# First stage of a one-core diffusion layer: order of the first loads, the split of the modulation product, and the first rows' high parts

## The chip, the cores and the metric

The kernel runs on one core of one Trainium2 chip. The metric is the device time of one execution in microseconds. The kernel before takes 2886.26 us in the median of three runs (2884.76 to 2886.59).

Names of the engines: PE is TensorE (matrix products and transposes through PSUM), DVE is VectorE, ACT is ScalarE, POOL is GpSimd, SP is the engine that only issues transfers (most loads here; ACT and POOL issue some as well). SBUF is the on-chip memory with 128 partitions, PSUM the accumulators that PE writes.

## What is computed

One layer of a diffusion backbone for 256 context tokens and 2048 latent tokens of width 1024, all in float32. Cut to what the first stage needs:

```python
def adaln(cvec, w_mod, b_mod):
    m = jax.nn.silu(cvec) @ w_mod + b_mod
    return jnp.split(m[:, None, :], 6, axis=-1)      # sh1, sc1, g1, sh2, sc2, g2

sh1, sc1, g1, sh2, sc2, g2 = adaln(c_ctx[None, :], w_mod[l], b_mod[l])
h = rms_norm(xp, norm1_g[l]) * (1 + sc1) + sh1
q, k, v, f = project(h, w_in[l], q_norm_g[l], k_norm_g[l])
...
sh1, sc1, g1, sh2, sc2, g2 = adaln(c, w_mod[l], b_mod[l])
h = rms_norm(xs, norm1_g[l]) * (1 + sc1) + sh1
```

`w_mod` is 1024 x 6144; the first 2048 of its columns give the shift and scale that stand ahead of the first projection. `w_in` is 1024 x 2048. After it come differential attention over 2560 keys, a Fourier mixing, an output projection and a squared-ReLU MLP; the change doesn't touch them.

## The kernel before

The tokens are 18 row blocks of 128; blocks 0 and 1 are the context. A float32 product is made from three faster ones: both operands are split into a high part (a cast to the type fp32r) and a low part (what the cast left), and high x high, high x low and low x high are accumulated (`mm3`, L88 to L90). The high part of W is cast by ACT, the low part subtracted by DVE.

The part that matters here is written by hand, in an order that the scheduler doesn't change (`tc.manual_schedule`, L437 to L547). Each engine and each issuing queue works through its own instructions in that order and stops at one whose inputs aren't there yet.

- `setup_small` (L92 to L110) loads the conditioning vectors c and c_ctx and the bias b_mod on SP's queue and the gains norm1_g, norm2_g and subln_g on ACT's, as rows of one tile; makes silu of the first 16 rows; transposes the tile on PE (L107) and copies it to `cols` (L108). `cols` then holds a column for each group of 128 values.
- `load(0)` brings row block 0 (X[0], 512 KB). Then come the eight pieces wm0 to wm7 of W_mod (L444), each 128 x 2048, 1 MB; X[1] is loaded between wm2 and wm3. ACT's queue also carries two pieces `rp` of the rotary table (L283), 64 KB each, which later stages use.
- `norm` (L204 to L212): square and row sum on ACT, the mean on DVE (nss, L209), the power -1/2 on POOL (nrs, L85), the scaling on DVE. Here of block 0; of block 1 at step 4 of the next loop.
- The transposes of block 0 on PE (L451), into two PSUM tiles of four.
- The modulation product, eight steps of k. PE multiplies the two columns of c and c_ctx with 1536 columns of wm_k (three products of 512, L455), and DVE sums the other 512 columns for each of the two vectors (L459 and L461), partition by partition.
- Six pieces of W, halves of 512 KB (L474), go where wm0 to wm2 were. There are 16 halves and six buffers, so the others are issued as the splitting frees buffers.
- The product's rows are copied from PSUM (L482) and transposed to columns (L484); sixteen products with a vector of ones (L489) sum DVE's part over the partitions. Bias (L492) and `mk_scale` (L201, L202) give `modc` and `scale1`. POOL loads the gains of q and k and the lambda vectors (L113, L116).
- Block 0 is modulated straight from its transposes in PSUM, the first tile by ACT (L502) and the second by DVE (L500), into SBUF; DVE then makes its high parts (L510) and low parts (L511). The transposes of block 1 follow on PE (L515).
- Projection of block 0: for each of eight k, ACT casts the four column groups of W (L523), DVE subtracts (L524), PE makes 12 products. On the side ACT modulates block 1 (L502, at k = 1 to 4), its high and low parts are made at k = 5 (L531, L532), and block 2 is normalised at k = 6; its transposes stand on PE within the last step (L221).
- Afterwards the four groups of block 0 are used (f: L402, v: L377, squares of q and k: L271) while PE projects block 1.

The pools of PSUM: `pj` has four tiles of 128 x 512 (the projection's groups, and the modulation product before them), `pt` two tiles for transposes, `pg` and `pm` one each.

## Time and profile before

| what | before |
|---|---|
| median of three runs | 2886.26 us (2884.76 to 2886.59) |
| the profiled execution's own time | 2886.51 us |
| its span in the trace | 2884.7 us |
| PE busy | 2847.6 us, 99% |
| DVE busy | 2011.5 us, 70% |
| ACT busy | 1547.0 us, 54% |
| POOL busy | 1061.7 us, 37% |
| moved by DMA | 492.93 MB, 171 GB/s over the span |

Times in the trace count from the start of the span. A row of the timeline gives start, duration (both us), engine, line, operation, output and inputs with their shapes, how many instructions were joined (x), and in brackets how long the engine had been idle before and what released it. A row of the groups gives line, engine and operation, then count, busy time in all (us), mean of one (ns), and idle time ahead of them with what ended most of it. A row of waits names the engine and line that waited, what for, us in total, times, and the longest.

### The profile page before, as it was taken

The page shows a single profiled execution, that of the slowest core. Times are in us where ns is not written, and L with a number is a line of the kernel's source. Part 1 is how long each engine was busy: PE and PEld are TensorE (multiplying, and loading weights), DVE is VectorE, ACT ScalarE, POOL GpSimd, SP SyncE. Part 2 cuts the span into 40 slices and gives each one's busy share as a digit, 9 for nine tenths or more (in the row PEclk, how much of TensorE's full clock was granted, in tenths as well). Part 3 has the DMA queues.
Part 4 walks back from the last instruction along what each step waited for, and adds up shares of the span by engine and source line. Part 5 has one row for each costly group of instructions (what it writes and reads, how often), then busy time and mean ns, then how long its engine had stood idle before and what let it go on. Part 6 is the DMA issues. An engine that isn't in the chain of part 4 may idle for free.

```text
span 2884.7 us, 43207 instructions
## 1 busy us (share of the span) xinstructions
PE 2847.6 (99%) x15119; PEld 2468.6 (86%) x15119; DVE 2011.5 (70%) x3375; ACT 1547.0 (54%) x3503; POOL 1061.7 (37%) x869
## 2 busy tenths in 40 slices
PE   8999999999999999999999999999999999999999
PEld 4888787688888888888889999999998888888887
DVE  6676776898988989865477777778775353345554
ACT  4333322798998989853356565556554332232221
POOL 1112112699999999942223333333332000000000
PEclk9999999999999999999999999999999999999999
DMA  7777888521211312037777677667747464345663
GB/s 283 202 201 190 227 210 231 195 106 43 73 69 45 114 38 98 21 112 208 236 219 233 219 247 229 220 218 238 232 166 254 146 201 137 133 143 185 200 206 110
DMA packets 392779, 492.93 MB, mean 171 GB/s; under 512 B 26467, under 2 KB 306384, under 8 KB 389490
## 3 DMA queue, kind: packets, MB, share of 16 engines
q1 hardware_dynamic: 387136, 479.73, 52.7%
q0 software_dynamic: 1872, 7.28, 0.7%
q10 hardware_dynamic: 3554, 3.17, 0.4%
q8 instruction: 119, 1.95, 0.3%
q14 instruction: 98, 0.80, 0.1%
HBM read 312.58 MB, written 179.59 MB: 171 GB/s over the span
## 4 chain that ended last, share of the span: by engine, by line
PE 91%; DVE 3%; ACT 3%; DMA 2%; issue 1%; POOL 0%; SPq 0%; ACTq 0%; DVEq 0%; POOLq 0%
PE Ss L1022 10%; PE ps L88 8%; PE ps L89 8%; PE ps L90 8%; PE pts L1077 5%; PE po L90 4%; PE po L88 4%; PE po L89 4%; PE pj L88 4%; PE pj L89 4%; PE pj L90 4%; PE pA L1685 2%; PE pA L1686 2%; PE pB L1685 2%; PE pB L1686 2%; PE pB L1687 2%
## 5 line engine op out<-in xcount | busy, mean ns | idle before, releaser
L1027 DVE TENSOR_REDUCE mxs<-Ss 128x1 f32<-128x512 f32 x636 | 413.3, 685 | 63.1 <-PE Ss L1022 52.0
L1362 DVE TENSOR_TENSOR sl<-sr,sh 128x768 fp32r<-128x768 f32 x168 | 161.7, 964 | 337.8 <-ACT sh L1361 337.3
L1062 POOL TENSOR_TENSOR P0s<-P0s,P1s 128x1024 f32<-128x1024 f32 (+2 forms) x128 | 378.7, 2958 | 10.7
L1361 ACT CAST sh<-sr 128x768 fp32r<-128x768 f32 x168 | 140.2, 836 | 424.8 <-PE ps L89 424.8
L1727 POOL TENSOR_TENSOR gs<-g,g 128x384 f32<-128x384 f32 x48 | 69.6, 1451 | 469.8 <-ACT g L1697 410.8
L1046 ACT ACTIVATE P1s<-Ss,mxs 128x512 f32<-128x512 f32 x318 | 215.2, 694 | 36.1 <-DVE mxs L1030 36.1
L88 PE MATMUL pj<-wh,hh 128*128 128x512 f32 x576 | 229.4, 398 | 3.9 <-DVE qn L289 3.2
L89 PE MATMUL ps<-tlT,sh 128*128 128x512 f32 x585 | 229.3, 392 | 0.0
L88 PE MATMUL ps<-thT,sh 128*128 128x512 f32 x585 | 229.0, 391 | 0.0
L89 PE MATMUL pj<-wl,hh 128*128 128x512 f32 x576 | 228.5, 397 | 0.5 <-DVE wl L524 0.5
L90 PE MATMUL ps<-thT,sl 128*128 128x512 f32 x585 | 227.7, 389 | 0.0
L90 PE MATMUL pj<-wh,hl 128*128 128x512 f32 x576 | 227.3, 395 | 0.0
L1046 ACT ACTIVATE P0s<-Ss,mxs 128x512 f32<-128x512 f32 x318 | 214.1, 691 | 5.5 <-DVE mxs L1030 4.9
L1022 PE MATMUL Ss<-KS1s,Qs 128*128 128x512 f32 x636 | 196.2, 420 | 6.2 <-ACT P0s L1046 3.5
L1022 PE MATMUL Ss<-KS0s,Qs 128*128 128x512 f32 x636 | 195.5, 420 | 2.4 <-ACT P1s L1046 2.4
L1077 PEld LDWEIGHTS pts<-ident,P0s 128*128 128x128 f32 x1280 | 157.7, 140 | 42.8 <-issue 2.1
L1077 PE MATMUL pts<-ident,P0s 128*128 128x128 f32 x1280 | 190.5, 272 | 0.7 <-ACT P1s L1046 0.7
L1696 ACT ACTIVATE g<-uz 128x384 f32<-128x384 f32 x144 | 75.8, 527 | 201.0 <-DVE uz L1719 171.3
L1061 POOL TENSOR_SCALAR P1s<-P1s,tots 128x1024 f32<-128x1024 f32 (+2 forms) x128 | 171.7, 1342 | 5.8
L1089 DVE TENSOR_TENSOR als<-pts,ahs 128x512 fp32r<-128x512 f32 x256 | 165.9, 681 | 6.8 <-ACT ahs L1084 6.6
L88 PE MATMUL ps<-ophT,sh 128*128 128x512 f32 x423 | 165.7, 392 | 1.1 <-DVE uz L1719 1.1
L90 PE MATMUL ps<-ophT,sl 128*128 128x512 f32 x423 | 165.7, 392 | 0.0
(531 smaller groups left out, 8056.3 us busy)
## 6 DMA issues: line engine op xcount, KB each, us to landing
sr<-sd SPq DMA_DIRECT2D x84, 768.0 KB
a<-in_w SPq DMA_DIRECT2D x184, 256.0 KB
sd<-gs SPq DMA_DIRECT2D x192, 192.0 KB
sd<-g SPq DMA_DIRECT2D x144, 192.0 KB
wm<-in_w_mod SPq DMA_DIRECT2D x32, 512.0 KB
Qs<-qd SPq DMA_DIRECT2D x32, 512.0 KB
b<-in_w SPq DMA_DIRECT2D x64, 256.0 KB
b<-tsum SPq DMA_DIRECT2D x64, 256.0 KB
```

The source lines that it names most:

```text
L88: nc.tensor.matmul(ps, lh, rh, start=first, stop=False)
L89: nc.tensor.matmul(ps, lh, rl, start=False, stop=False)
L90: nc.tensor.matmul(ps, ll, rh, start=False, stop=last)
L1022: nc.tensor.matmul(S[:, :w], self.Q[:, x, m, j * P:j * P + P], self.hd.KS[m][:, b * 512:b * 512 + w], start=(x == 0), stop=(x == 1))
L1027: nc.vector.tensor_reduce(self.mx[j][:, m, b:b + 1], self.S[j, m, b], axis=AX.X, op=ALU.max)
L1046: nc.scalar.activation(dst, S, AF.Exp, bias=self.mx[j][:, m, 6:7], accum_out=self.sm[j][:, m, b:b + 1])
L1061: nc.gpsimd.tensor_scalar(p, p, tot[:, 3:4], 0.0, op0=ALU.mult, op1=ALU.add)
L1062: nc.gpsimd.tensor_add(d, d, p)
L1077: nc.tensor.transpose(pt[:, c:c + P], self.p0[j][:, (kb + t) * P:(kb + t + 1) * P], ident)
L1089: nc.vector.tensor_sub(t, self.pt[kb], f32(self.A[kb][0]))
L1361: nc.scalar.copy(hi, src)
L1362: nc.vector.tensor_sub(lo, src, f32(hi))
```

## The change

W_mod's first two pieces lead SP's queue, x0 comes behind them, and x1 behind the second half of W. c and c_ctx are loaded on ACT's queue and are transposed by themselves (16 rows, `setup_cond`); the bias and the gains are loaded afterwards, on ACT's queue too (`load_rows`), and transposed after step 1 of the modulation product (`setup_rows`). Block 0 is normalised at step 2 and transposed at steps 3 to 6, block 1 normalised in the second stage, at step 1.

In the modulation product PE takes 1280 columns of each piece (512, 512, 256) and DVE 768. DVE's sums are reduced by two transposing reduces, and four products with shifted identity blocks (`quads`, which a later stage used already) finish the sum over the partitions, where sixteen products with ones stood.

ACT casts the four groups of W's first piece, and DVE subtracts the first, ahead of the scale. For block 0, `h_first` lets ACT write the high part straight from PSUM and DVE write the whole value to SBUF from the same PSUM tile, then subtract; the first tile ahead of the projection's loop, the second at its step 1. Block 1's transposes are made in two fours after steps 1 and 3, its modulation is at steps 2 to 5, its split at step 6. Block 2 is loaded at step 4 and normalised at step 7. In the last step the groups go 3, 2, 0, 1.

```diff
@@ -89,23 +89,33 @@
-        def setup_small(pool, pps):
+        def load_cond(pool):
             rows = pool.tile([P, P], F32, tag="t2", name="rows", bufs=6)
             nc.vector.memset(rows, 0.0)
-            nc.sync.dma_start(rows[0:8, :], a["c"].rearrange("o (r p) -> (o r) p", p=P))
-            nc.sync.dma_start(rows[8:16, :], a["c_ctx"].rearrange("(r p) -> r p", p=P))
-            nc.sync.dma_start(rows[32:80, :], a["b_mod"].rearrange("o (r p) -> (o r) p", p=P))
-            nc.scalar.dma_start(rows[80:88, :], a["norm1_g"].rearrange("o (r p) -> (o r) p", p=P))
-            nc.scalar.dma_start(rows[88:96, :], a["norm2_g"].rearrange("o (r p) -> (o r) p", p=P))
-            nc.scalar.dma_start(rows[96:97, :], a["subln_g"])
+            nc.scalar.dma_start(rows[0:8, :], a["c"].rearrange("o (r p) -> (o r) p", p=P))
+            nc.scalar.dma_start(rows[8:16, :], a["c_ctx"].rearrange("(r p) -> r p", p=P))
+            return rows
+        def setup_cond(pool, pps, rows):
             e = pool.tile([16, P], F32, tag="t2", name="e", bufs=6)
             nc.scalar.activation(e, rows[0:16, :], AF.Exp, scale=-1.0)
             nc.vector.tensor_scalar_add(e, e, 1.0)
             nc.vector.reciprocal(e, e)
             nc.vector.tensor_mul(rows[0:16, :], rows[0:16, :], e)
+            pr = pps.tile([P, 16], F32, tag="pg", name="prc")
+            nc.tensor.transpose(pr, rows[0:16, :], ident[0:16, 0:16])
+            nc.vector.tensor_copy(cols[:, 0:16], pr)
+        def load_rows(rows):
+            nc.scalar.dma_start(rows[32:80, :], a["b_mod"].rearrange("o (r p) -> (o r) p", p=P))
+            nc.scalar.dma_start(rows[80:88, :], a["norm1_g"].rearrange("o (r p) -> (o r) p", p=P))
+            nc.scalar.dma_start(rows[88:96, :], a["norm2_g"].rearrange("o (r p) -> (o r) p", p=P))
+            nc.scalar.dma_start(rows[96:97, :], a["subln_g"])
+        def setup_rows(pps, rows):
             pr = pps.tile([P, P], F32, tag="pg", name="pr")
             nc.tensor.transpose(pr, rows, ident)
-            nc.vector.tensor_copy(cols, pr)
+            nc.vector.tensor_copy(cols[:, 32:97], pr[:, 32:97])
             nc.vector.tensor_scalar_mul(cols[:, 96:97], cols[:, 96:97], 1.0 - LAM_INIT)
...
@@ -169,13 +179,17 @@
-        def mod_sums(t2, pps, sums, gi):
-            z = t2(f"quad{gi}")[:, 0:224]
+        def quads(t2, nm):
+            z = t2(nm)[:, 0:224]
             nc.gpsimd.memset(z, 0.0)
             nc.gpsimd.tensor_add(z[:, 96:128], ident[:, 0:32], ident[:, 32:64])
             for q in (2, 3):
                 nc.gpsimd.tensor_add(z[:, 96:128], z[:, 96:128], ident[:, 32 * q:32 * q + 32])
+            return z
+        def mod_sums(t2, pps, sums, gi):
+            z = quads(t2, f"quad{gi}")
             FIN[gi] = pm = pps.tile([P, 4, 2, 4], F32, tag="pm", name=f"pm{gi}")
             for q in range(4):
                 nc.tensor.matmul(pm, z[:, 96 - 32 * q:224 - 32 * q], sums[:, :, :, q::4], start=(q == 0), stop=(q == 3))
@@ -436,31 +450,36 @@
             with tc.manual_schedule():
                 with tc.tile_pool(name="p0r", bufs=3) as rows, tc.tile_pool(name="p0m", bufs=KD - 3, side="right") as more:
-                    setup_small(p1, pps)
-                    load(0)
+                    rw = load_cond(p1)
                     wm = []
                     for k in range(KD):
                         wm.append((rows if k < 3 else more).tile([P, 2048], F32, tag="row", name=f"wm{k}"))
                         nc.sync.dma_start(wm[k], wmod[:, k, 0:2048])
-                        if k == 2:
-                            load(1)
-                    norm(p1, X[0], "a0")
-                    pr = [pp.tile([P, 512], F32, tag="pj", name=f"pr{gi}", bufs=4) for gi in range(4)]
+                        if k == 1:
+                            load(0)
+                    setup_cond(p1, pps, rw)
+                    load_rows(rw)
+                    z = quads(t2, "quad0")
+                    pr = [pp.tile([P, 512], F32, tag="pj", name=f"pr{gi}", bufs=4) for gi in range(3)]
                     pt0 = [pp.tile([P, 4, P], F32, tag="pt", name=f"pta0_{b}") for b in range(2)]
+                    acc = [f32(p1.tile([P, KD, P], F32R, tag=f"h{x}", name=f"macc_{x}")).rearrange("p k t -> p (k t)")[:, 0:768] for x in "hl"]
                     for k in range(KD):
-                        nc.tensor.transpose(pt0[k // 4][:, k % 4, :], X[0][:, k * P:(k + 1) * P], ident)
-                    acc = [t2(f"macc3_{s}") for s in range(2)]
-                    for k in range(KD):
-                        for gi in range(3):
-                            nc.tensor.matmul(pr[gi][0:2, :], cols[:, k:k + 9:8], wm[k][:, gi * 512:gi * 512 + 512], start=(k == 0), stop=(k == KD - 1))
+                        for gi, w in enumerate((512, 512, 256)):
+                            nc.tensor.matmul(pr[gi][0:2, :w], cols[:, k:k + 9:8], wm[k][:, gi * 512:gi * 512 + w], start=(k == 0), stop=(k == KD - 1))
                         for s in range(2):
-                            wk, sc = wm[k][:, 1536:2048], cols[:, 8 * s + k:8 * s + k + 1]
+                            wk, sc = wm[k][:, 1280:2048], cols[:, 8 * s + k:8 * s + k + 1]
                             if k == 0:
                                 nc.vector.tensor_scalar_mul(acc[s], wk, sc)
                             else:
                                 nc.vector.scalar_tensor_tensor(acc[s], wk, sc, acc[s], op0=ALU.mult, op1=ALU.add)
-                        if k == 4:
-                            norm(p1, X[1], "a1")
+                        if k == 1:
+                            setup_rows(pps, rw)
+                        if k == 2:
+                            norm(p1, X[0], "a0")
+                        if 3 <= k < 7:
+                            for x in (2 * k - 6, 2 * k - 5):
+                                nc.tensor.transpose(pt0[x // 4][:, x % 4, :], X[0][:, x * P:(x + 1) * P], ident)
+                    X.pop(0)
...
@@ -473,67 +492,85 @@
                         wraw.append(halves.tile([P, 1024], F32, tag="half", name=f"win{k}_{h}"))
                         nc.sync.dma_start(wraw[n], wsrc[:, k, h * 1024:h * 1024 + 1024])
+                    def w_raw(k, g):
+                        return wraw[2 * k + g // 2][:, g % 2 * 512:g % 2 * 512 + 512]
+                    def w_high(k, g):
+                        nc.scalar.copy(wh[g][k], w_raw(k, g))
+                    def w_rest(k, g):
+                        nc.vector.tensor_sub(wl[g][k], w_raw(k, g), f32(wh[g][k]))
+                        if g % 2 and 2 * k + g // 2 + 6 < 16:
+                            w_half(2 * k + g // 2 + 6)
                     for n in range(6):
                         w_half(n)
-                    pm = pps.tile([P, 16, 2], F32, tag="pg", name="pm16")
-                    def mod_cols(gi):
+                        if n == 1:
+                            load(1)
+                    pm = pps.tile([P, 10, 2], F32, tag="pg", name="pm10")
+                    pq = pps.tile([P, 2, 6], F32, tag="pm", name="pm6")
+                    sums = t2("sums0")[:, 0:48].rearrange("p (s c) -> p s c", s=2)
+                    for s in range(2):
+                        nc.vector.tensor_reduce(sums[:, s, :], acc[s].rearrange("p (c i) -> p c i", i=32), axis=AX.X, op=ALU.add,
+                                                apply_transpose=True)
+                    for gi in range(3):
+                        w = 256 if gi == 2 else 512
                         r = t2(f"mr{gi}")
-                        (nc.vector.tensor_copy if gi == 1 else nc.scalar.copy)(r[0:2, :], pr[gi][0:2, :])
-                        for j in range(4):
+                        nc.scalar.copy(r[0:2, :w], pr[gi][0:2, :w])
+                        for j in range(w // P):
                             nc.tensor.transpose(pm[:, gi * 4 + j, :], r[0:2, j * P:(j + 1) * P], ident[0:2, 0:2])
-                    mod_cols(0)
-                    for s in range(2):
-                        for j in range(4):
-                            nc.tensor.matmul(pm[:, 12 + j, s:s + 1], acc[s][:, j * P:(j + 1) * P], ones, start=True, stop=True)
-                    mod_cols(2)
-                    mod_cols(1)
-                    nc.vector.tensor_add(modc[:, 0:16, :], pm, cols[:, 32:48].unsqueeze(2).to_broadcast([P, 16, 2]))
+                    for q in range(4):
+                        nc.tensor.matmul(pq, z[:, 96 - 32 * q:224 - 32 * q], sums[:, :, q::4], start=(q == 0), stop=(q == 3))
+                    for g in range(4):
+                        w_high(0, g)
+                    w_rest(0, 0)
+                    nc.vector.tensor_add(modc[:, 0:10, :], pm, cols[:, 32:42].unsqueeze(2).to_broadcast([P, 10, 2]))
+                    nc.vector.tensor_add(modc[:, 10:16, :], pq.rearrange("p s j -> p j s"), cols[:, 42:48].unsqueeze(2).to_broadcast([P, 6, 2]))
                     mk_scale(scale1, 8, 80)
                     lq = load_gains(p1)
                     HH.update({i: tuple(p1.tile([P, KD, P], F32R, tag=f"h{x}", name=f"h{x}{i}") for x in "hl") for i in range(2)})
...
                     h0 = [t2(f"hTa0_{b}").rearrange("p (k t) -> p k t", k=4) for b in range(2)]
-                    for k in range(4):
-                        h_mod(h0[0][:, k, :], pt0[0], k, nc.scalar)
-                        h_mod(h0[1][:, k, :], pt0[1], 4 + k, nc.vector)
-                    for b in range(2):
+                    def h_first(b):
+                        for k in range(4 * b, 4 * b + 4):
+                            sc, sh = scale1[:, k, 1:2], modc[:, k, 1:2]
+                            nc.scalar.activation(HH[0][0][:, k, :], pt0[b][:, k % 4, :], AF.Identity, bias=sh, scale=sc)
+                            nc.vector.tensor_scalar(h0[b][:, k % 4, :], pt0[b][:, k % 4, :], sc, sh, op0=ALU.mult, op1=ALU.add)
                         hi, lo = (x[:, b * 4:b * 4 + 4, :] for x in HH[0])
-                        nc.vector.tensor_copy(hi, h0[b])
                         nc.vector.tensor_sub(lo, h0[b], f32(hi))
-                    X.pop(0)
-                    pt1 = [pp.tile([P, 4, P], F32, tag="pt", name=f"pta1_{b}") for b in range(2)]
-                    for k in range(KD):
-                        nc.tensor.transpose(pt1[k // 4][:, k % 4, :], X[1][:, k * P:(k + 1) * P], ident)
-                    X.pop(1)
+                    h_first(0)
                     PJ.update({(0, g): pp.tile([P, 512], F32, tag="pj", name=f"pj0_{g}", bufs=4) for g in (3, 2, 0, 1)})
                     hT = p1.tile([P, KD, P], F32, tag="hT", name="hTa1", bufs=1)
-                    load(2)
+                    pt1 = [None] * 2
                     for k in range(KD):
                         for g in range(4):
-                            w = wraw[2 * k + g // 2][:, g % 2 * 512:g % 2 * 512 + 512]
-                            nc.scalar.copy(wh[g][k], w)
-                            nc.vector.tensor_sub(wl[g][k], w, f32(wh[g][k]))
-                            if g % 2 and 2 * k + g // 2 + 6 < 16:
-                                w_half(2 * k + g // 2 + 6)
-                        if 1 <= k < 5:
-                            for x in (2 * k - 2, 2 * k - 1):
-                                h_mod(hT[:, x, :], pt1[x // 4], x, nc.scalar)
-                        if k == 5:
+                            if k:
+                                w_high(k, g)
+                            if k or g:
+                                w_rest(k, g)
+                        if k == 1:
+                            h_first(1)
+                            norm(p1, X[1], "a1")
+                        if k == 4:
+                            load(2)
+                        if 2 <= k < 6:
+                            for x in (2 * k - 4, 2 * k - 3):
+                                nc.scalar.activation(hT[:, x, :], pt1[x // 4][:, x % 4, :], AF.Identity, bias=modc[:, x, 1:2], scale=scale1[:, x, 1:2])
+                        if k == 6:
                             nc.scalar.copy(HH[1][0], hT)
                             nc.vector.tensor_sub(HH[1][1], hT, f32(HH[1][0]))
-                        if k == 6:
+                        if k == 7:
                             norm(p1, X[2], "a2")
-                        for g in range(4):
+                        for g in (3, 2, 0, 1) if k == KD - 1 else range(4):
                             mm3(PJ[0, g], HH[0][0][:, k, :], HH[0][1][:, k, :], wh[g][k], wl[g][k], k == 0, k == KD - 1)
+                        if k in (1, 3):
+                            b = k // 2
+                            pt1[b] = pp.tile([P, 4, P], F32, tag="pt", name=f"pta1_{b}")
+                            for x in range(4):
+                                nc.tensor.transpose(pt1[b][:, x, :], X[1][:, (4 * b + x) * P:(4 * b + x + 1) * P], ident)
+                            if b:
+                                X.pop(1)
```

6 lines of the change are left out of this document (removed).

## The prediction

> **What bounds the kernel now.** First the page: TensorE is busy all through, so whatever shifts its work in the first stage shifts the end.
>
> ```profile
> span 2884.7 us, 43207 instructions
> PE 2847.6 (99%) x15119; PEld 2468.6 (86%) x15119; DVE 2011.5 (70%) x3375; ACT 1547.0 (54%) x3503; POOL 1061.7 (37%) x869
> ...
> PE 91%; DVE 3%; ACT 3%; DMA 2%; issue 1%; POOL 0%; SPq 0%; ACTq 0%; DVEq 0%; POOLq 0%
> ```
>
> Only the first 66 us differ in the changed kernel; after some 210 TensorE instructions its order there is the same. Does later slack swallow a shift? TensorE's waits after 66 us say hardly:
>
> ```profile
> PE pj L88 <- DVE qn L289: 3.2, 3, 2.1
> ...
> PE Ss L1022 <- ACT P0s L1046: 1.7, 2, 1.0
> ...
> PE pz L701 <- DVE ys L714: 1.5, 1, 1.5
> ```
>
> The seven rows of that view from 66 to 560 us, of which these are the largest (us in total, times, longest), sum to 8.5 us. So the question is when TensorE gets to the first product of row block 1. Next, the chain of waits and the windows of this stretch (columns of a window: us, then busy us of PE, PEld, DVE, ACT, POOL with counts, granted clock, DMA share, GB/s):
>
> ```profile
> 10.98 21.73 PE pr L455 x48
> ...
> 10.90:32.70 21.80, 21.80 (x50) 4.15 (x50) 11.31 (x17) 1.72 (x3) 4.10 (x7) 1.00 1.01 372
> ...
> 38.20:44.00 5.80, 5.28 (x17) 4.05 (x16) 5.77 (x10) 5.80 (x14) 0.00 (x0) 0.52 0.29 102
> ...
> 43.75:61.67 17.92, 17.92 (x78) 1.00 0.75 270
> ```
>
> Two stages: the modulation products, bound by TensorE (2.72 us for each of 8 steps) with the load nearly as long; then projection 0, where TensorE starts at half clock and afterwards makes a product every 17.92/78 = 0.23 us (the last row is of those products alone). The border between the stages and the second one's end are in the timeline:
>
> ```profile
> 35.55 0.19 DVE L492 TENSOR_TENSOR modc<-pm,cols 128x32 f32<-128x32 f32 x1 [2.98 <-PE pm L484]
> ...
> 35.98 0.17 DVE L202 TENSOR_TENSOR scale<-scale,cols 128x16 f32<-128x16 f32 x1
> ...
> 36.19 1.50 ACT L502 ACTIVATE hTa<-pta,modc,scale 128x128 f32<-128x128 f32 x4 [2.87 <-DVE scale L202]
> 36.26 1.36 DVE L500 TENSOR_SCALAR hTa<-pta,scale,modc 128x128 f32<-128x128 f32 x4
> ...
> 62.02 2.49 DVE L524 TENSOR_TENSOR wl<-win,wh 128x512 fp32r<-128x512 f32 x4
> ...
> 62.16 1.09 PE L221 MATMUL pta<-ident,x 128*128 128x128 f32 x8 [0.32 <-DVE x L212]
> ...
> 65.39 0.40 PE L90 MATMUL pj<-wh,hl 128*128 128x512 f32 x1
> ...
> 66.47 0.51 PE L88 MATMUL pj<-wh,hh 128*128 128x512 f32 x1 [0.69 <-ACT fo L402]
> ```
>
> Call S the end of scale1: 35.98 + 0.17 = 36.15. Projection 0 ends at 65.79, which is S + 29.6; the first product of block 1 starts at 66.47, 0.69 of it spent waiting for fo.
>
> **First stage: the new S.** Per step TensorE streams 512 + 512 + 256 columns where it streamed three times 512, 2.72 x 5/6 = 2.27 us. For the loads and for VectorE's 768 columns in place of 512:
>
> ```profile
> 2.21 0.45 SPq L247 DMA_DIRECT2D x<-in_x_prompt  x1
> ...
> 5.69 1.06 ACT L208 ACTIVATE nsqa<-x 128x1024 bf16<-128x1024 f32 x1 [0.82 <-DMA x<-in_x_prompt]
> ...
> 17.53 1.42 DVE L461 SCALAR_TENSOR_TENSOR macc<-wm,cols,macc 128x512 f32<-128x512 f32 x2 [2.35 <-DMA wm<-in_w_mod]
> ...
> 20.01 1.41 DVE L461 SCALAR_TENSOR_TENSOR macc<-wm,cols,macc 128x512 f32<-128x512 f32 x2 [1.07 <-DMA wm<-in_w_mod]
> ...
> L1362 DVE TENSOR_TENSOR sl<-sr,sh 128x768 fp32r<-128x768 f32 x168 | 161.7, 964 | 337.8 <-ACT sh L1361 337.3
> ...
> L524 DVE TENSOR_TENSOR wl<-win,wh 128x512 fp32r<-128x512 f32 x32 | 19.9, 686 | 2.1 <-ACT wh L523 2.1
> ```
>
> A piece of W_mod lands each 2.48 us (17.53 to 20.01, both starts released by one). x0, half a piece, was asked for at 2.21 and there at 5.69, 3.5 later; wm0, asked for about 0.75 now that the three row loads ahead of SP's stream are gone, is there 1.25 after such a time, at 5.5; wm1 follows at 8, x0 at 9.3, wm2 at 11.8, wm3 at 14.3, wm7 at 24.2.
>
> From 512 to 768 columns costs 964 - 686 = 278 ns, so a step is 2 x (0.66 + 0.28) = 1.88 us. (0.66 is an estimate for ops in a row: a pair alone takes 1.42, and the subtractions of the same size, 686 ns singly, follow each other at 0.614 in a row quoted below.) This alone would hide under the load. What doesn't hide are the small loads. As built, every hardware load takes one of eight completion semaphores in turn and isn't issued before its predecessor on that semaphore has landed. Before has one such wait, and it is long:
>
> ```profile
> SPq L444 <- DMA rp<-in_rope: 4.8, 1, 4.8
> ...
> 3.35 0.36 ACTq L283 DMA_DIRECT2D rp<-in_rope  x1
> ...
> 10.98 0.33 SPq L444 DMA_DIRECT2D wm<-in_w_mod  x1
> ...
> q1 hardware_dynamic: 251, 1.79, 96.2%
> q10 hardware_dynamic: 144, 0.07, 5.1%
> ...
> 1.53 1.66 DMA rows<-in_c_ctx
> ```
>
> (The two q rows are the DMA queues in 6.5 to 11 us; in 3.4 to 6.5 the ACT queue, q10, has no packet.) So a 64 KB load on ACT's queue, issued at 3.35 while SP's stream of W_mod filled the DMA engines, moved nothing for 3.15 us and landed at 10.96, after 7.6; on an idle machine a row load took 1.66. In the changed kernel b_mod, the two gains and subln stand on ACT's queue behind that stream, and wait in turn for x0, the rope piece, wm2 and wm3 to land. subln is issued at 14.3 then and lands between 14.3 + 1.7 = 16.0 and 14.3 + 7.6 = 21.9. I take 18.4 (4.1 later): its one packet should behave as the rope load's first, 3.15 us or somewhat more. Queued behind it: TensorE's transpose in setup_rows stands in order between steps 1 and 2, and VectorE's copy of it ahead of step 2's sums. Both engines stop. TensorE alone would be there at about 16.5: c_ctx at 5.9 (the 3.2 of before plus such a delay of 2.7), 4.1 us of silu and transpose (1.53 + 1.66 to 6.99 + 0.29, below), then two steps, mostly at half clock.
>
> ```profile
> 6.99 0.29 DVE L108 COPY cols<-pr 128x128 f32<-128x128 f32 x1 [0.58 <-PE pr L107]
> ...
> 60.45 0.15 DVE L209 TENSOR_SCALAR nssa<-nssa 128x1 f32<-128x1 f32 x1
> ...
> 61.35 0.75 DVE L212 TENSOR_SCALAR x<-x,nrsa 128x1024 f32<-128x1024 f32 x1 [0.75 <-POOL nrsa L85]
> ...
> L167 DVE TRANSPOSE_TENSOR_REDUCE sums<-macc 128x16 f32<-128x512 f32 x2 | 1.4, 700 | 0.0
> ```
>
> So with the rows' transpose (0.4) VectorE restarts at 18.8, and now sets the stage: 0.4 for the two row ops; step 2, 1.88; norm(x0), moved in here, 0.90 from nssa to x (60.45 to 61.35) and 0.67; steps 3 to 7, 9.4; two transposing reduces at 700 + 278 ns, less their overlap, 1.9; four quad products and hand-offs about 0.95 (from 0.65 for the eight small transposes of before to 1.95 for its sixteen ones-products); modc to scale1 0.60 and one added 0.1. Sum 16.8, S = 35.6, half a microsecond sooner than before, not the three that the lighter products offer. The x0 transposes, mr copies and mr transposes lie under VectorE's steps; TensorE's own steps from 18.8 would end near 33, so their cover is some 2 us. The quads on GpSimd run in its idle time (4.10 busy of 21.80); the memset, the silu on 16 rows and the gains' loads change nothing that anything waits for. W's halves take the place of wm0 to wm2, free at step 2's end (20.7), behind wm7's load (24.2), and x1 comes behind the second of them, near 28, 15 us ahead of its norm; without that cover its lateness would count in full.
>
> **Second stage.** ACT has cast four pieces of W ahead, VectorE subtracted one. But h_first has ACT and VectorE read the same PSUM tile, and in the built program each op waits for the other engine's previous one. Before, the two engines worked on two tiles at once (36.19 and 36.26). Price of a round, from the means of single ops, and other prices:
>
> ```profile
> L502 ACT ACTIVATE hTa<-pta,modc,scale 128x128 f32<-128x128 f32 x12 | 4.7, 457 | 2.9 <-DVE scale L202 2.9
> ...
> L500 DVE TENSOR_SCALAR hTa<-pta,scale,modc 128x128 f32<-128x128 f32 x4 | 1.4, 404 | 0.1
> ...
> 38.19 0.69 DVE L511 TENSOR_TENSOR hl<-hTa,hh 128x512 fp32r<-128x512 f32 x1
> ...
> 39.86 9.82 DVE L524 TENSOR_TENSOR wl<-win,wh 128x512 fp32r<-128x512 f32 x16
> ...
> 56.90 1.23 DVE L532 TENSOR_TENSOR hl<-hTa,hh 128x1024 fp32r<-128x1024 f32 x1
> ...
> 58.84 1.07 ACT L208 ACTIVATE nsqa<-x 128x1024 bf16<-128x1024 f32 x1
> ```
>
> 457 + 404 + two hand-offs of 40 (36.15 to 36.19) = 0.94, four rounds 3.76 where the pair took 1.5. The Trainium skill, "PSUM — Partial Sum Buffer", section "PSUM bank collisions raise a hardware error", says that two engines may not read one bank in the same partitions at once, so that software has to keep them apart. By that rule a block costs 3.76; without it the 1.5 would stand, and the sum would be 2 x 2.26 lower. No row of before has two engines on one tile.
>
> VectorE's chain from S: h_first(0) 3.76, its low part 0.69, 31 subtractions at 9.82/16 = 0.614 (19.03), h_first(1) 3.76 and 0.69, norm(x1), which moved here, 2.1 (ACT's square of 1.07 + 0.2 less the 0.69 beside it, then 0.90 and 0.67), x1's low part 1.23: 31.3. Then the last step takes group 3 first, whose low piece VectorE makes last, and 11 products follow: 2.5. End at S + 33.8. TensorE by itself: S + 4.5, 96 x 0.23, 2.3 for its cold start, about 2.8 for the hole where x1's transposes wait behind h_first(1) and norm(x1), 0.9 for them: S + 32.6; so VectorE leads by a little. In before VectorE was done with the last piece at 62.02 + 2.49 = 64.51, S + 28.4, and TensorE 1.3 later; there VectorE also waited for pieces still loading, which in the changed kernel have 3 us more time from the start of the stage (h_first) to come. x2's load, now after W's last piece, is needed only at step 7 (some 2 us of cover).
>
> **The sum.** E = 35.6 + 33.8 = 69.4. x2's transposes leave this stretch and come after block 1, 0.87 to be added (1.09, some 0.2 of it beside the next product); the wait for fo is gone, as group 3 ends first. 69.4 + 0.87 - 66.47 = +3.8 us. Profiled execution: 2886.51, of which 1.8 outside the span; it lies inside the runs (2884.76 to 2886.59), 0.25 above their median. 2886.5 + 3.8 = 2890.3, 0.14% slower.
>
> **Rivals.**
> A, small loads land 1.7 us after issue as c_ctx did: VectorE restarts at 16.4, S = 33.2, +1.4, 2887.9. For it: subln is one packet; against: the rope load. The Trainium skill, "DMA: Bandwidth & Descriptors", section "Queues, rings and completion order", has each DMA engine switch between queues packet by packet; by that rule a load of one packet isn't held up by the stream. The rope load's 3.15 us without a packet speaks against it.
> B, faster: A's early rows and, in the second stage, ACT and VectorE overlapping on the tile after all, with no hole before x1's transposes; then it lasts 29.6 as before: 33.2 + 29.6 - 65.79 - 0.69 = -3.7, 2882.8. It decides below about 31.5 us from S to E. Against: the waits in the program.
> C, subln takes the rope load's 7.6: 21.9, restart 22.3, S = 39.1, +7.3, 2893.8; TensorE idle for 5 us would add a cold start, as in the window at clock 0.52.
> D, the shift is partly hidden in later slack: the 3.2 us that TensorE waits for qn are used up, +0.6, 2887.1.
>
> **Chances.** Forecast 50% (its own range 2888.5 to 2892), A 20, C 17, B 8, D 5. The range 2884 to 2895.5 leaves out B and C's tail. 0.2%, about what a measurement of this kernel can tell from no change, is 5.8 us: slower by more holds for C and the forecast's upper edge with an S above 37.6, 30%; faster by more only for B with a stage still 2 us shorter, 6%; within, 64%.
>
> **What would show it.** A stop of TensorE and VectorE between steps 1 and 2 released by the subln load, its end near 18.4 (16: A; 22: C). Scale1's end at 35.6. ACT and VectorE alternating on pta at 0.94 us a round. TensorE idle 2 to 3 us before x1's transposes, and S to the last product of block 0 near 33.8. The forecast is wrong if the stop is missing, if the alternation costs under 0.6 a round, or if the first product of block 1 shifts by 4 and the end doesn't.

## The result, and the profile after

The changed kernel takes 2903.3 us (median of four runs, 2902.83 to 2903.58) where the kernel before took 2885.81 in the same runs: a ratio of 1.0061, 95% interval 1.0043 to 1.0078. It is 17.5 us slower; 3.8 were forecast, and the range ended at 2895.5. The profiled execution grew by 16.7 us. The page of the changed kernel, in its lines that answer to those shown of before:

```profile
span 2901.4 us, 43208 instructions
PE 2853.3 (98%) x15110; PEld 2466.0 (85%) x15110; DVE 2016.5 (69%) x3380; ACT 1549.4 (53%) x3508; POOL 1063.1 (37%) x873
PE 90%; DVE 3%; ACT 3%; DMA 2%; issue 1%; POOL 0%; SPq 0%; ACTq 0%; DVEq 0%; POOLq 0%
```

TensorE was busy 5.7 us longer (2853.3 against 2847.6) with nine instructions less, and idle 11 us longer. The first sign that the first stage isn't all of it: instructions of equal work got slower. To see where, the same instruction is looked up in both timelines. Here those of before behind the projections (two transposes and a product of the Fourier part), then the same of the changed kernel, with the last of scale1 and the first product of block 1 ahead of them:

```profile
309.11 0.50 PE L88 MATMUL pj<-wh,hh 128*128 128x512 f32 x1 [2.08 <-DVE qn L289]
...
495.92 0.60 PE L848 MATMUL pt<-ident,qo 128*128 128x128 f32 x4
...
502.38 0.33 PE L754 MATMUL pabp<-c,fps 128*128 128x65 f32 x2
```

```profile
39.14 0.17 DVE L216 TENSOR_TENSOR scale<-scale,cols 128x16 f32<-128x16 f32 x1
...
74.71 0.39 PE L88 MATMUL pj<-wh,hh 128*128 128x512 f32 x1
...
508.68 0.60 PE L885 MATMUL pt<-ident,qo 128*128 128x128 f32 x4
...
519.93 0.33 PE L791 MATMUL pabp<-c,fps 128*128 128x65 f32 x2
```

| point | before | changed | shift |
|---|---|---|---|
| end of scale1 (S) | 36.15 | 39.31 | 3.2 |
| first product of block 1 | 66.47 | 74.71 | 8.2 (9.1 with the transposes of x2 that are still to come, 0.87) |
| last transposes of q and k | 495.92 | 508.68 | 12.8 |
| first product with fps | 502.38 | 519.93 | 17.55 |
| end of the span | 2884.7 | 2901.4 | 16.7 |

So the shift has three parts: 9.1 us in the part that the prediction spoke of, some 4 more that grow over 400 us in which TensorE's order is the same in both kernels, and nearly 5 at one place at 500 us.

**The steady part.** The windows of 72 products in a row without a gap (us, busy us of PE and count, granted clock, DMA share, GB/s; products of the projection alone), first of before, then of the changed kernel:

```profile
150.68:167.16 16.48, 16.48 (x73) 1.00 0.87 225
```

```profile
161.03:177.83 16.80, 16.80 (x73) 1.00 0.84 222
```

16.48/72 = 0.2289 us a product, and 16.80/72 = 0.2333, at the same granted clock and with the same instructions. Some 1,600 products have this spacing, and 1,600 x 0.0044 is 7 us. Not all of it is left at 496 us, as the waits differ too, most of all at 309 us, where the shift falls by 2.1. TensorE waits for qn there, 2.08 us in before (the row above) and 1.50 in the changed kernel. Behind the wait before's products run at half clock for 3.4 us and the changed kernel's don't. The windows of 4.3 us from the first product on, of before and of the changed kernel (all columns):

```profile
309.10:313.40 4.30, 4.29 (x12) 3.41 (x13) 4.30 (x10) 0.00 (x0) 0.00 (x0) 0.60 0.95 217
```

```profile
321.00:325.30 4.30, 4.29 (x18) 3.49 (x19) 4.30 (x10) 0.00 (x0) 0.00 (x0) 1.00 0.90 206
```

**The jump.** The changed kernel's timeline at 504 us:

```profile
503.76 0.68 DVE L830 TENSOR_TENSOR d<-ss,ss 128x512 f32<-128x512 f32 x1
...
505.50 0.56 SPq L392 DMA_DIRECT2D vs<-vo  x1
...
508.81 1.90 DVE L830 TENSOR_TENSOR d<-ss,ss 128x512 f32<-128x512 f32 x3 [4.37 <-issue]
...
515.62 2.07 PE L738 MATMUL pz<-abo,cw 128*128 128x512 f32 x2 [2.90 <-DVE qkT_1l L645]
```

VectorE stops for 4.37 us between the first and the second of four subtractions, and the profile names no releaser ("issue"). In the kernel before the four follow each other. Their inputs had landed by 504 us. What the built program adds here is a wait for a later transfer: the second subtraction writes d1024_2, which lies at 29472 bytes of each partition, and in the changed kernel vo17 lies there too, whose store SP issued at 505.50. Before, vo17 was at 19232. t2 has six slots that its tiles use in turn, and another order of a few tiles in the first stage is carried through 450 us to this place. TensorE's wait of 2.90 us is not the whole jump of 4.8: behind it TensorE runs at half clock for 3.4 us, which costs it about 1.7 more.

```profile
515.50:518.90 3.40, 3.28 (x4) 1.46 (x5) 1.67 (x4) 0.58 (x1) 2.36 (x5) 0.50 0.75 178
```

**The first 70 us.** The chain of waits of the changed kernel, then its timeline, then its windows:

```profile
15.59 4.43 DMA rows<-in_subln_g
20.40 6.08 PE pr L468 x12
26.85 2.24 PE pr L468 x6
...
40.29 0.47 ACT hh L537
...
41.23 0.47 ACT hh L537
...
42.16 0.47 ACT hh L537
```

```profile
20.07 0.33 PE L117 MATMUL pr<-ident,rows 128*128 128x128 f32 x1 [3.29 <-DMA rows<-in_subln_g]
...
20.44 0.23 DVE L118 COPY cols<-pr 128x65 f32<-128x65 f32 x1 [6.52 <-PE pr L117]
...
53.43 0.66 PE L571 MATMUL pta<-ident,x 128*128 128x128 f32 x4 [2.36 <-DVE x L226]
...
72.05 0.50 PE L89 MATMUL pj<-wl,hh 128*128 128x512 f32 x1 [1.09 <-DVE nssa L223]
```

```profile
20.00:25.00 5.00, 4.93 (x9) 1.05 (x10) 3.86 (x7) 0.00 (x0) 2.15 (x4) 0.66 1.00 415
...
55.00:58.00 3.00, 3.00 (x9) 2.33 (x8) 3.00 (x6) 3.00 (x7) 0.00 (x0) 0.50 0.67 216
```

The stop of both engines for subln is there (3.29 and 6.52 us idle), the alternation is there (rounds start 0.94 apart), and so is the hole before x1's transposes (2.36). What the prediction hadn't in its sum is the clock: after the stop two steps took 6.08 us (2.24 each at full clock), and after the hole TensorE ran at 0.50 once more. Not every execution of these instructions lost that time, as the experiments show.

### The profile page after: what moved, and what is told of

Same layout as the page of the kernel before. It is cut to its first block, busy times and chain, and to the rows that moved or that the text cites. A ratio compares the mean times of both kernels' runs of the same rounds, so it can differ in the third digit from the quotient of the medians.

```text
span 2901.4 us, 43208 instructions
## 1 busy us (share of the span) xinstructions
PE 2853.3 (98%) x15110; PEld 2466.0 (85%) x15110; DVE 2016.5 (69%) x3380; ACT 1549.4 (53%) x3508; POOL 1063.1 (37%) x873
## 4 chain that ended last, share of the span: by engine, by line
PE 90%; DVE 3%; ACT 3%; DMA 2%; issue 1%; POOL 0%; SPq 0%; ACTq 0%; DVEq 0%; POOLq 0%
PE Ss L1059 10%; PE ps L88 8%; PE ps L89 8%; PE ps L90 8%; PE pts L1114 5%; PE pj L88 4%; PE pj L89 4%; PE pj L90 4%; PE po L90 4%; PE po L88 4%; PE po L89 4%; PE pA L1722 2%; PE pA L1723 2%; PE pB L1722 2%; PE pB L1723 2%; PE pB L1724 2%
## 5 line engine op out<-in xcount | busy, mean ns | idle before, releaser
L90 PE MATMUL pj<-wh,hl 128*128 128x512 f32 x576 | 229.3, 399 | 3.2 <-DVE hl L540 3.2
L89 PE MATMUL ps<-tlT,sh 128*128 128x512 f32 x585 | 229.3, 392 | 0.0
```

The source lines that it names most:

```text
L89: nc.tensor.matmul(ps, lh, rl, start=False, stop=False)
L90: nc.tensor.matmul(ps, ll, rh, start=False, stop=last)
```

## The experiments

Times are medians; kernels that stand in one group of runs share the runs of before. Runs of one kernel lie within 2.5 to 6.3 us of each other (the four of the changed kernel within 0.8), and each kernel was profiled once, so a profile can lie some us from its kernel's median.

**Placement.** Three kernels that move memory and hardly an instruction. In the changed kernel VectorE's sums have the tags of hh and hl, so these two get their memory ahead of nsq and ff. `a1_place` names those tags first:

```diff
+                    for t, shape, dt, n in (("nsq", [P, D], mybir.dt.bfloat16, 1), ("nss", [P, 1], F32, 2), ("nrs", [P, 1], F32, 2), ("ff", [P, 512], F32, 4)):
+                        p1.tile(shape, dt, tag=t, name=f"{t}_first", bufs=n)
                     acc = [f32(p1.tile([P, KD, P], F32R, tag=f"h{x}", name=f"macc_{x}"))...
```

> The changed kernel with one thing undone: the tiles hh and hl lie at 50080 to 66464 bytes of each partition again, as before the change, not at 39712 to 56096; no instruction is added or taken. Theory (placement): the pitch of the projection's products goes back from 0.2333 to 0.2297 us, so the shift against before no longer grows between 70 and 490 us (3.7 us net, 5.6 where slack didn't absorb it); the first 70 us and the jump at 500 us stay: about 2898 to 2900 where the changed kernel takes 2903.3. Rival 1 (the pitch hangs on the order of the PSUM tiles, or on the clock after another start): the pitch stays at 0.2333 and the time at 2903. Rival 2 (the pitch is noise of one execution): 2903 as well, with either pitch.

`b1_place` is the kernel before with hh and hl named ahead of the rest:

```diff
                     load(0)
+                    for x in "hl":
+                        p1.tile([P, KD, P], F32R, tag=f"h{x}", name=f"h{x}_first")
```

> The kernel before with nothing changed but the memory of hh and hl: 39712 to 56096 bytes, where the changed kernel has them. Theory (placement): the products' pitch rises from 0.2297 to 0.2333 us, 3.7 to 5.6 us by 490 us: 2889.5 to 2891.5 where before takes 2885.8. Rivals (PSUM order, clock, noise): 2885.8, pitch 0.2297.

`b3_hh` does so for hh alone. In all three kernels nsq and ff lie elsewhere too, b1_place included, so hh and hl aren't the only tiles that were moved; the projection's products read neither nsq nor ff.

> The kernel before with only the tiles of hh moved to 39712 to 47904 bytes, nsq and ff behind them; hl stays at 58272 as before. Of three products two have hh as their stationary operand. Theory (each product pays for where its own stationary tile lies): products with hh at 0.2333 us, those with hl at 0.2297, two thirds of b1_place's loss: about 2889. Rival 1 (the pitch is a common one and set by both tiles' distance, or by hl): 2885.7, all products at 0.2297. Rival 2 (hh alone decides): all at 0.2333, 2891.

Measured: a1_place 2900.53, b1_place 2891.14, before 2885.33 beside both; b3_hh 2889.18 beside 2885.72. b1_place is 1.0020 of before (1.0010 to 1.0029), b3_hh 1.0012 (1.0002 to 1.0021). The windows of the same 72 products, of a1_place, b1_place and b3_hh:

```profile
156.61:173.09 16.48, 16.48 (x73) 1.00 0.88 224
```

```profile
151.77:168.57 16.80, 16.80 (x73) 1.00 0.84 221
```

```profile
152.34:169.04 16.70, 16.70 (x73) 1.00 0.85 223
```

The spacing follows the memory both ways: 0.2289 with the old place, 0.2333 with the new, in either kernel. b3_hh has 0.2319, two thirds of the way, and two of three products have hh as their stationary operand; as a sum this is what the theory said, though not product by product. In its trace (means of all such pairs from 100 to 480 us) the next start comes 235.3 ns after a product with hl, 231.2 from one product with hh to the next, and 229.3 from hh to hl. Only starts of products with hh are late, which speaks for the place of the stationary operand and against nsq and ff. What it is about these addresses that costs 4 ns wasn't found out.

b1_place loses 5.8 us by tiles that were moved, without an instruction added. Its profile doesn't lay all of that to the spacing: the shift against before is 2.8 us at the first product with fps, and 4.6 at the end. 1.6 of the rest come in one stretch at half clock at 566 us, which before's profile doesn't have and whose cause is open:

```profile
566.20:569.70 3.50, 3.50 (x11) 2.71 (x12) 1.61 (x3) 3.03 (x9) 3.42 (x3) 0.51 0.15 57
```

The time of a1_place fell by a little less than expected, and the waits of its TensorE say why:

```profile
PE pz L740 <- DVE qkT_1l L647: 4.4, 1, 4.4
```

It comes to the store of vo17 earlier and waits there 4.4 us in place of 2.9, and behind that it runs at a clock of 0.51 from 508 to 515 us, twice as long as the changed kernel.

**Reuse.** `a2_rotate` puts the 48 reduced sums into a slot of ff, so that t2 rotates otherwise and vo17 comes to lie at 21280:

```diff
-                    sums = t2("sums0")[:, 0:48].rearrange("p (s c) -> p s c", s=2)
+                    sums = p1.tile([P, 512], F32, tag="ff", name="sums0", bufs=4)[:, 0:48].rearrange("p (s c) -> p s c", s=2)
```

> The changed kernel with its reduced sums in another pool slot (ff in place of t2), so that vo17, 450 us later, falls on other memory than d1024_2. Theory (reuse): in the changed kernel VectorE stops 4.4 us at 504 us because d1024_2 is written where vo17's store still reads; here that stop is gone, TensorE's wait of 2.9 us for the product pz goes with it, and the shift against before doesn't jump from 12.8 to 17.5 us: about 2898.5. Rival (the stop is a code fetch or a busy DMA queue; the profile names no releaser): it stays, 2903.3.

2897.74 beside 2885.33, 5.6 us under the changed kernel (5.1 if each is taken against its own before), and the four subtractions follow each other again:

```profile
500.84 2.49 DVE L830 TENSOR_TENSOR d<-ss,ss 128x512 f32<-128x512 f32 x4
```

TensorE's wait for pz is gone from the view of waits there. The stop was a wait for a store, not a code fetch.

`c1_both` joins the two.

> The changed kernel with both placements undone: hh and hl at 50080 to 66464 bytes and the reduced sums in slot ff, so that vo17 and d1024_2 lie apart. Theory: the two effects are separate, the pitch is 0.2297 us and VectorE doesn't stop at 504 us; what is left is the shift of the first 70 us (5.5 to 9 us in the profiles so far) less some 2 us that the slack at 305 us takes: 2890 to 2893 where before takes 2885.5. Rival (the two share a cause, such as one busy DMA stretch): no better than the better of the two alone, 2897 to 2898.

2892.4 beside 2885.74 (1.0023, 1.0013 to 1.0032). So of 17.5 us some 11 go with the placement, and 6.7 are left, for which the first two stages have to answer. The following kernels start from c1_both and look into these.

**The late rows.** `a3_rows` (from the changed kernel) calls load_rows right behind load_cond.

> The changed kernel with the loads of b_mod, norm1_g, norm2_g and subln_g issued right behind c_ctx, ahead of the silu. Theory (late rows): TensorE and VectorE no longer stop between steps 1 and 2 (3.3 and 6.5 us in the changed kernel); TensorE goes from step 1 to step 2 at about 17 us and its eight steps set the stage, scale1 ends near 35 to 36 in place of 39.3, and the time falls by 3 to 4 us: about 2899.5. Rival (W_mod's pieces or VectorE's sums set the stage, the stop is hidden): scale1 stays within 1 us of 39.3, the time within 1 us of 2903.3.

A miss: 2902.91 beside 2885.33, though the stop is gone. Its timeline:

```profile
7.24 0.26 ACTq L113 DMA_DIRECT2D rows<-in_subln_g  x1
...
8.88 1.28 ACT L101 ACT_TABLE_LOAD   x1 [8.88 <-DMA rows<-in_b_mod]
...
12.64 7.06 PE L468 MATMUL pr<-wm,cols 128*2 128x512 f32 x12 [0.27 <-DVE cols L107]
...
19.63 0.33 PE L117 MATMUL pr<-ident,rows 128*128 128x128 f32 x1
```

Now the silu waits on ACT behind the four loads (8.88 where the changed kernel had 7.17), so step 0 starts 1.7 us later, and steps 0 and 1 take 7.06 us, mostly at half clock, where two at full clock take 4.5. TensorE is at step 2 at 19.89, against 20.33. Scale1 ends at 37.2, 2.1 us before the changed kernel's, but a1_place and a2_rotate, which have the changed kernel's instructions, had 37.4 and 37.7 in their profiles: the gain is no more than what executions differ by. The loads had to come off the path, not to another place on it.

`c2_rows` therefore issues all six ahead of W_mod, c, c_ctx and b_mod on SP:

```diff
-            nc.scalar.dma_start(rows[0:8, :], a["c"].rearrange("o (r p) -> (o r) p", p=P))
...
+            nc.sync.dma_start(rows[0:8, :], a["c"].rearrange("o (r p) -> (o r) p", p=P))
...
+            nc.scalar.dma_start(rows[96:97, :], a["subln_g"])
...
-                    load_rows(rw)
```

> c1_both with all six small loads ahead of W_mod, c, c_ctx and b_mod on SP's queue as before the change, W_mod behind them and x0 behind its second piece. Theory (late small loads): the columns are there near 7.3 us in place of 10.9, TensorE has the first step from about 8 us and doesn't stop after step 1; scale1 ends at 32 to 34 in place of 37 to 39, and the time is 4 to 5 us under c1_both. Rival (after a3_rows: TensorE at half clock and VectorE's sums set the stage whatever the loads do): scale1 within 1 us of c1_both's, the time too.

Another miss: 2891.36 beside 2885.74, 1.0 us under c1_both. In its profile the columns were there at 7.0, and still scale1 ended at 39.35. That execution took 2895.82 us, 4.5 over the median, with the clock at 0.50 from 29.8 to 46.8, so it says little about size; but TensorE waited 3.96 us in it for the last piece of W_mod, a wait that c1_both doesn't have. c4_all, below, shows the reason more plainly.

**The collision.** `c3_pair` lets ACT and VectorE work on different PSUM tiles and swap, `c4_all` joins that with c2_rows and brings the last step's casts into the order of its products.

```diff
+                    def h_first():
+                        for b in range(2):
+                            for j in range(4):
+                                k, n = 4 * b + j, 4 * (1 - b) + j
+                                nc.scalar.activation(HH[0][0][:, k, :], pt0[b][:, j, :], AF.Identity, bias=modc[:, k, 1:2], scale=scale1[:, k, 1:2])
+                                nc.vector.tensor_scalar(h0[1 - b][:, j, :], pt0[1 - b][:, j, :], scale1[:, n, 1:2], modc[:, n, 1:2], op0=ALU.mult, op1=ALU.add)
```

> c1_both with h_first for both tiles ahead of the loop, ACT on one PSUM tile while VectorE is on the other, then swapped: the same 16 ops, no alternation on one tile. Theory (alternation): eight rounds take about 3.2 us in place of 2 x 3.75, TensorE's hole before x1's transposes (2.4 us) closes, and from scale1's end to the first product of block 1 it takes 30 to 31 us in place of 34 to 35; the time is 3 to 4 us under c1_both. Rival (TensorE's half clock and the casts of W set the second stage): within 1 us of c1_both.

> c1_both with the small loads first (c2_rows), the paired h_first (c3_pair), and the last step's casts and subtractions in the order of its products (3, 2, 0, 1). Theory: the three add up, scale1 ends at 32 to 34, block 1 starts at about 62 to 64 where before has 66.5, and the kernel is faster than before: 2881 to 2884. Rival (the two stages are both bound by TensorE's half clock after its pauses): 2886 to 2889, no better than before.

c3_pair: 2889.95 beside 2885.74, 2.5 us under c1_both, a little less than expected; from scale1's end to block 1 it took 32.2 us (33.7 in c1_both, 30 to 31 expected). Its timeline has the 16 ops in 2.9 us:

```profile
37.26 2.91 ACT L540 ACTIVATE hh<-pta,modc,scale 128x128 fp32r<-128x128 f32 x8
37.26 1.37 DVE L541 TENSOR_SCALAR hTa<-pta,scale,modc 128x128 f32<-128x128 f32 x4
...
38.79 1.37 DVE L541 TENSOR_SCALAR hTa<-pta,scale,modc 128x128 f32<-128x128 f32 x4 [0.17 <-ACT hh L540]
```

c4_all: 2885.11 beside 2885.74, no difference (0.9999, 0.9990 to 1.0009), where 2881 to 2884 was expected. Its timeline shows what both kernels with early rows ran into:

```profile
19.80 1.06 POOL L124 DMA_DIRECT2D lq<-in_lambda_k  x2
...
31.54 3.65 PE L467 MATMUL pr<-wm,cols 128*2 128x512 f32 x6 [3.06 <-DMA wm<-in_w_mod]
31.58 1.02 DVE L473 SCALAR_TENSOR_TENSOR macc_h<-wm,cols,macc_h 128x768 f32<-128x768 f32 x1 [3.79 <-DMA wm<-in_w_mod]
...
37.60 0.17 DVE L214 TENSOR_TENSOR scale<-scale,cols 128x16 f32<-128x16 f32 x1
```

The last piece of W_mod came only at 31.5. POOL's six loads of the gains stand behind norm(x0)'s power; as everything was earlier, they were issued by 21 us, into the last pieces of W_mod. `d1_gains` issues them behind norm(x1):

```diff
-                    lq = load_gains(p1)
...
                             norm(p1, X[1], "a1")
+                            lq = load_gains(p1)
```

> c4_all with one thing moved: the six loads of the gains of q and k and of the lambda vectors on POOL's queue are issued behind norm(x1), at the second step of the projection. Theory (collision): in c2_rows and c4_all these loads, issued at 17 to 21 us since VectorE and POOL were early, moved in the same stretch as wm7, which landed at 31.5 us in place of 25; here wm7 lands near 25, TensorE's wait of 3 us for it and VectorE's of 3.8 go, scale1 ends at 32 to 34 in place of 37.8, and the time is 3.5 to 4.5 us under c4_all's 2885.1: about 2881, faster than before. Rival (wm7 is late because W's halves behind it share its stream): wm7 still lands near 31, 2885.

2882.45 beside 2885.57, 2.7 us under c4_all, a little less than expected. Its timeline, wm7 there in time and scale1 5.9 us earlier, of which 3.6 are left where block 1 starts:

```profile
27.14 2.31 PE L467 MATMUL pr<-wm,cols 128*2 128x512 f32 x6
...
31.74 0.18 DVE L214 TENSOR_TENSOR scale<-scale,cols 128x16 f32<-128x16 f32 x1
...
63.08 0.39 PE L88 MATMUL pj<-wh,hh 128*128 128x512 f32 x1
```

Block 1 starts at 63.08 (66.47 in before), and the time is the lowest of all kernels here, 0.9993 of before; the interval, 0.9984 to 1.0002, just holds 1, so that it beats before, by 2 to 3 us, is likely and not certain.

`d3_rowsgains` is c2_rows with the same move; it asks what the rows cost of themselves.

> c2_rows with the same move of the gains' loads: against c1_both it has the small loads first, and nothing that collides with W_mod. Theory (late small loads cost, and c2_rows hid it behind the collision): scale1 ends at 32.5 to 34.5 where c1_both has 37.2, and the time is 3 to 4.5 us under c1_both's 2892.4: 2888 to 2889. Rival (the stop between steps 1 and 2 costs nothing of itself): 2892.

2886.73 beside 2885.57, 5.7 us under c1_both, with scale1 ending at 31.6: the late rows cost more than was thought, once nothing takes their place.

`d2_casts` (d1_gains with ACT's four casts ahead of the copies of the product's rows, and the low-part products of step 0 last):

> d1_gains with two more: ACT casts W's first piece ahead of the copies of the product's rows, and in the projection's first step TensorE makes the products with the high part of x0 first and those with its low part last. Theory: TensorE's wait of 2.4 us for the low part goes and its half clock falls on products that it would wait for anyway; 1 to 2 us under d1_gains. Rival (VectorE's chain sets the second stage): within 0.5 us of d1_gains.

A miss: 2884.92, 2.5 us over d1_gains (their intervals against before overlap). Its view of waits shows what got worse:

```profile
PE pm L522 <- ACT mr L520: 1.5, 1, 1.5
```

ACT waits for W's first half and casts while the product's rows stand ready, so scale1 ends at 33.7; from there to block 1 it takes as long as in d1_gains (31.1 us), so no gain of the other order of step 0 is seen.

## Why the prediction was wrong

The sign was right and the size wrong by a factor of more than four. Step by step:

- **"Only the first 66 us differ in the changed kernel; after some 210 TensorE instructions its order there is the same."** This step failed. The order was the same, the memory was not. Two new tiles in the tags of hh and hl, and another order of tiles in t2, moved what the next 450 us work on. Putting hh and hl ahead of nsq and ff costs 5.8 us (b1_place), not all of it seen in the spacing; the store to wait for, with the half clock behind it, costs 5.1 to 5.6 (a2_rotate). No rival had this in it. With both undone (c1_both) the time is 2892.4, 6.7 us over before, and lies within the range.
- **Restart after subln, 18.4 plus 0.4.** The mechanism was right, and the size nearly: subln was issued at 15.59 (14.3 in the sum) and landed 4.43 us later (4.1 in the sum), so VectorE restarted at 20.44 instead of 18.8. The Trainium skill, "DMA: Bandwidth & Descriptors", section "Queues, rings and completion order", lets an engine change between queues packet by packet; the row of 4.43 us for a load of 512 bytes doesn't agree with rival A, which followed from it.
- **S = 35.6, with VectorE setting the stage.** This step failed too. S was 39.31. 1.6 us of it are the restart, and the rest is TensorE, which the sum had 2 us out of the way: its half clock after the stop made two steps last 6.08 us. In a2_rotate, with the same first stage, steps 0 and 1 took 7.20 us in place of 5.85, so the pause was shorter; the clock stayed at 1.00 behind it, and scale1 ended at 37.7. There too VectorE had its reduces done at 35.3, and modc waited for TensorE, whose last step ended at 35.3 and the small products behind it at 37.1. A row of a2_rotate's timeline, and one of its windows:

```profile
20.18 0.33 PE L117 MATMUL pr<-ident,rows 128*128 128x128 f32 x1 [2.27 <-DMA rows<-in_subln_g]
```

```profile
20.00:24.00 4.00, 3.82 (x11) 1.00 (x12) 2.75 (x6) 0.00 (x0) 1.04 (x2) 1.00 1.02 422
```

The Trainium skill, "TensorE: Matmul & The Clock Gate", section "Part 1: The HAM clock gate", gives half clock after an idle window of about 3.4 us that runs free. The rows here don't agree: TensorE's half clock also came behind waits of 2.36 us (the hole before x1's transposes) and 2.08 us (before, at 309 us), where it had been busy for 1.29 and 1.33 of the last 3.41 us; behind waits of 2.27 us (a2_rotate) and 1.50 us (the changed kernel, at 321 us) it didn't come. Rival C had named a cold start, for a longer pause.
- **Second stage, S + 33.8.** 74.71 - 39.31 = 35.4. The alternation at 0.94 a round, the hole of 2 to 3 us (2.36) and the last step's wait for group 3 were all there; the cold start after the hole (3 us at clock 0.50) was not in the sum. In a1_place, a2_rotate and c1_both, with the same instructions in this stage, the clock read 1.00 there, and the stretch took 34.3, 33.8 and 33.7 us: for these the sum was right. How often the clock falls in either place isn't known.
- **"TensorE's waits after 66 us say hardly."** The shift fell by 2.1 us at 309 us, less than rival D's 3.2, and only 0.6 of that is a shorter wait; the rest is the half clock that before had there. That the slack is small held.
- **The chances.** Slower by more than 0.2% had 30%, on grounds (late rows, rival C) that bear on the part up to block 1 alone.

## What to carry to other kernels

A change in one stage is also a change in where every later tile lies. Compare the addresses and the waits of the two built programs behind the stage that was edited, and if they differ, name the tags in the old order first; only then does a time say something of the edit.

Moving loads earlier moves them into other loads. Here six small loads that nobody waited for cost 5.9 us of the first stage, and 2.7 of the whole time, as soon as POOL came to them sooner. Look for what each freed engine issues next.

In the built program two engines that read one PSUM tile take turns; give each its own tile and swap (2.9 us in place of 7.5 for 16 ops, 2.5 of the whole time).

## What was not expected of the hardware

The spacing of equal products depends on where the stationary operand lies in SBUF: 228.9 ns with hh and hl at 50080 to 66464 bytes, 233.3 at 39712 to 56096, 231.9 with hh moved and hl not. Which property of the addresses decides was not tried.

The granted clock reads 1.00 at the start of these traces although TensorE is slow there: in the changed kernel steps 0 and 1 took 5.85 us, and two steps at full clock take 4.5 (the second row is of one step). Until the first change is recorded, the durations tell the clock, not the column. Nor does one profile tell where the clock will fall in the next: S was 39.31 in the changed kernel's, and 37.2 to 37.7 in those of a1_place, a2_rotate and c1_both with the same instructions up to there.

```profile
10.93 5.85 PE L468 MATMUL pr<-wm,cols 128*2 128x512 f32 x12 [0.27 <-DVE cols L107]
...
32.00 2.31 PE L468 MATMUL pr<-wm,cols 128*2 128x512 f32 x6
```
